# Diagonal blocks packed by ScalarE and sent in one transfer, a shorter layer norm, and a new rule of the planner, in a two-layer trunk on one core

## The chip, the cores and the metric

The kernel runs on one core of a Trainium2 chip. A core has five engines that run their own instruction queues: TensorE (PE, matmuls; PEld is its weight load), VectorE (DVE), ScalarE (ACT), GpSimd (POOL) and SyncE (SP), which here only issues transfers between DRAM and on-chip memory. The metric is the device time of one execution in microseconds (us). The kernel before takes 2513.36 us, the median of three runs of 2513.36, 2511.43 and 2513.53 us.

## What is computed

A decoder trunk of two layers on a sequence of 1024 positions of width 1024, in fp32. Layer 0 mixes the positions by a gated DeltaNet of 8 heads (width 128), layer 1 by an S5 state-space scan. Beside each mixer runs a 4-head attention into 256 memory vectors, and an MLP with squared ReLU follows:

```python
for i in range(DEPTH):                       # 2
    mix, xq = gdn_mixer(x, ...) if i == 0 else s5_mixer(x, ...)
    h = jnp.concatenate([mix, memory_attention(xq, mem, w_kv_mem[i])], -1) @ w_o[i]
    x = layer_norm(DN_ALPHA * x + h, ln1_g[i], ln1_b[i])
    f = jnp.square(jax.nn.relu(x @ mlp_w1[i])) @ mlp_w2[i]
    x = layer_norm(DN_ALPHA * x + f, ln2_g[i], ln2_b[i])

def layer_norm(x, g, b):
    mu = jnp.mean(x, -1, keepdims=True)
    var = jnp.mean(jnp.square(x - mu), -1, keepdims=True)
    return (x - mu) * lax.rsqrt(var + LN_EPS) * g + b

# gated DeltaNet, for one head and chunk by chunk:
#   a_strict = strictly lower part of (beta k) k^T * decay
#   sol = (I + a_strict)^-1 [beta v, beta k exp(gc)]
#   v_new = u - w S ;  o = (q exp(gc)) S + (q k^T * decay) v_new ;  S = S exp(g) + k_dec^T v_new
#   o = o * rsqrt(mean(o^2) + RMS_EPS) * norm_g * silu(z)
```

## The kernel before

**Shape of the work.** A sequence is 8 tiles of 128 positions. Large products use three matmuls per step, high by high, low by high and high by low halves (lines 397, 398 and 399), with the halves made by ScalarE (line 363, 900) and VectorE (line 364, 901). The mixer of layer 0 runs head by head, each head in two halves of four tiles (`hf` is 0 or 1), while the projections of the next heads (tiles `wi`, `wz`, lines 397 to 399) fill TensorE.

**N^T and its transfers.** For each head and half `gdn_keys_out` makes the 128-wide strictly triangular matrices N^T of four tiles (tile `NT`, line 1160: minus the key products times the decay). GpSimd sends the four 32-wide diagonal blocks to DRAM tensor `ntd` with four transfers (line 1163) and the whole tile to `ntf` with one (line 1164). That is 16 calls.

**The inverse.** For each pair of heads `gdn_inverse` loads diagonal blocks back in another layout, solves them in small steps and ends with a run of 16 VectorE instructions on 512 elements (lines 1233 and 1235, in the helper `prod`, called here "the burst"). It reads tiles `X` and `st`, whose loads are lines 1225 to 1227, on SyncE. GpSimd sends the result out (lines 1245, 1246). `gdn_invert_tiles` loads pieces of it per head through SyncE and GpSimd (lines 1272, 1275, 1279) and finishes the 128-wide inverse (tile `iv`) on TensorE (line 1284).

**The recurrence.** `gdn_recur` then steps through the eight tiles of a head. One step is a chain over three engines: `ks` (PE, line 1429), `R` (DVE, line 1431), `pe` (PE, line 1435, needs `iv`), `e` (ACT copy, line 1437), `pS` (PE, line 1441), `S` (DVE, line 1446). Next to it the output of the step is gathered in `po` (PE, lines 1432 and 1447), of which there is one buffer. At the end of a half ScalarE sums the squares (line 1455), VectorE adds a term (line 1456), GpSimd raises to the power -1/2 (line 1457), and ScalarE scales `po` into `on` (line 1460). Only then can the first `po` matmul of the next half be issued. `e`, `R` and `S` share six buffers of one size (tag "S").

**Layer norm.** `layer_norm` either takes statistics by VectorE (lines 509 and 510) or by ScalarE (lines 502 and 505, with small VectorE steps 503 and 506); line 511 makes 1024 (variance + 1e-5), GpSimd raises that to the power -1/2 (line 512), and two passes of VectorE over the tile finish it (lines 522 and 523; lines 514 and 517 for the last tile, which is sent out in two halves by line 518). As the power carries a factor 1/32, the scale vector was multiplied by 32 on ScalarE beforehand (line 2346). In the last MLP the partial sums of a tile are added by line 938.

**What sets the order.** After the program is written down, a planner (`settle`) lists all instructions of all engines in a new order: it keeps a clock per engine and a table of costs and, step by step, takes the instruction that can start first, with preference for the one whose due time is earliest. An instruction becomes ready when those that it depends on are done by the planner's clock, with a lag. Its order is fixed into every engine's queue, in which instructions start in order. So a change of any instruction's cost, engine or dependence moves others on all engines.

Of the kernel before, what the change touches and what calls it, by code (L numbers as in the profile page):

```python
# [10 lines left out]
F32 = mybir.dt.float32  # L11
F32R = mybir.dt.float32r
AF = mybir.ActivationFunctionType
ALU = mybir.AluOpType
AX = mybir.AxisListType

P = 128
# [16 lines left out]
class Trunk:  # L34
    def __init__(self, ctx, tc, a):
        self.tc = tc
        self.nc = nc = tc.nc
        self.a = a
        self.uid = 0
        self.turn = 0  # L40
        self.proj = 0
        self.soon = set()
        self.home, self.fixed = {}, set()
        self.cp = ctx.enter_context(tc.tile_pool(name="cp", bufs=1))
        self.sp = ctx.enter_context(tc.tile_pool(name="sp", bufs=1))
        self.ps = ctx.enter_context(tc.tile_pool(name="ps", bufs=1, space=bass.MemoryType.PSUM))
        self.dp = ctx.enter_context(tc.tile_pool(name="dp", bufs=1, space=bass.MemoryType.DRAM))
        self.ident = self.const("ident", [P, P])
        make_identity(nc, self.ident)
        self.const("pad", [P, 112])  # L50
        self.eps_ln = self.const("eps_ln", [P, 1])
        nc.gpsimd.memset(self.eps_ln, 1024 * 1e-5)
        self.mhalf = self.const("mhalf", [P, 4])
        nc.gpsimd.memset(self.mhalf, -0.5)
        self.half = self.const("half", [P, 4])
        nc.gpsimd.memset(self.half, 0.5)
# [5 lines left out]
    def settle(self, first, last, reach=0.0, ahead=15.0, passes=1, margin=0.0, late=0.0, hold=1e3):  # L62


        E = mybir.EngineType
# [7 lines left out]
        ins = traced[k0:k1]  # L73
        n = len(ins)
# [38 lines left out]
        deps = [set() for _ in ins]  # L113
        reads, writes, users, fresh, cost, port = {}, {}, {}, [], [], []
        opened, follow = {}, [set() for _ in ins]
        for x, i in enumerate(ins):
            new, big, shared = [], 1, i.engine in (E.DVE, E.Pool)
            for out, side in ((False, i.ins), (True, i.outs)):
                for q in side:
# [4 lines left out]
                    b = box(ap)  # L124
# [52 lines left out]
        lag = 0.05  # L177
# [3 lines left out]
        for _ in range(passes):  # L181
# [36 lines left out]
            while len(order) < n:  # L218
# [24 lines left out]
                r, x = first_[1:]  # L243
# [21 lines left out]
                    slots[t].remove(min(slots[t]))  # L265
                    turn[t].remove(nm)
                for y in after[x] + then[x]:
                    same = e == E.PE and ins[y].engine == e
                    ready[y] = max(ready[y], r + (0.0 if x not in deps[y] else busy if same else length + lag + (margin if ins[y].engine == E.PE else 0.0)))
                    wait[y] -= 1  # L270
                    if not wait[y]:
                        open_[ins[y].engine].append(y)
# [220 lines left out]
    def layer_norm(self, y, gb, junk=None, last=None):  # L493
# [1 line left out]
        nc = self.nc  # L495
        st = self.tile("st", [P, 2, 6], F32, "bn")
        halves = y if isinstance(y, list) else [y[:, c * HALF:(c + 1) * HALF] for c in range(2)]
        mv = self.tile("st", [P, 4], F32, "mv")
        if junk is not None:
            s = st.rearrange("p a b -> p (a b)")  # L500
            for c in range(2):
                nc.scalar.activation(junk, halves[c], AF.Copy, accum_out=s[:, c:c + 1])
            nc.vector.tensor_scalar(mv[:, 0:1], s[:, 0:1], s[:, 1:2], -1.0 / 1024, op0=ALU.add, op1=ALU.mult)
            for c in range(2):
                nc.scalar.activation(junk, halves[c], AF.Square, bias=mv[:, 0:1], accum_out=s[:, 4 + c:5 + c])
            nc.vector.scalar_tensor_tensor(mv[:, 2:3], s[:, 4:5], s[:, 5:6], self.eps_ln, op0=ALU.add, op1=ALU.add)
        else:
            for c in range(2):
                nc.vector.bn_stats(st[:, c, :], halves[c])
            nc.vector.bn_aggr(mv[:, 0:2], st)  # L510
            nc.vector.tensor_scalar(mv[:, 2:3], mv[:, 1:2], 1024.0, 1024 * 1e-5, op0=ALU.mult, op1=ALU.add)  # L511
        nc.gpsimd.tensor_tensor(mv[:, 3:4], mv[:, 2:3], self.mhalf[:, 0:1], op=ALU.pow)  # L512
        if last is not None:
            nc.vector.scalar_tensor_tensor(y, y, mv[:, 0:1], gb[0], op0=ALU.subtract, op1=ALU.mult)
            for c in range(2):
# [611 lines left out]
    def gdn_keys_out(self, h, hf):  # L1127
# [28 lines left out]
        for t in range(4):  # L1156
            tt = 4 * hf + t
            c = slice(tt * P, (tt + 1) * P)
            nc.tensor.matmul(pq[:, t, :], kT[:, c], kT[:, c], start=True, stop=True)
        V.scalar_tensor_tensor(n, pq, -1.0, d, op0=ALU.mult, op1=ALU.mult)  # L1160
        for b in range(4):
            q = slice(32 * b, 32 * b + 32)
            nc.gpsimd.dma_start(self.ntd[h, t4, b].rearrange("t j i -> j t i"), n[q, :, q])
        nc.gpsimd.dma_start(self.ntf[h, hf], n)

    def gdn_inverse(self, h0):
# [1173 lines left out]
    def mlp_block(self, i, B, ahead, xd, side, out, more):  # L2340
        new = []

        def done(y, tau):
            if tau == 0:
                self.gb2 = self.load_gb(self.a["ln2_g"][i:i + 1], self.a["ln2_b"][i:i + 1])
                self.nc.scalar.activation(self.gb2[0], self.gb2[0], AF.Copy, scale=32.0)
                if more:
                    new.extend(self.new_xT())
            self.layer_norm(y[tau], self.gb2, self.psum("mm", "jk") if tau in ((), (5, 6))[i] else None, last=out[tau] if tau == 7 and not more else None)
            if tau < 7 or more:  # L2350
                self.nc.sync.dma_start(out[tau], y[tau])
            if more and tau == 7:
                self.last_x(y, new, more(new))
            elif more and tau < 6:
                self.transpose_x(y[tau], tau, new)

        self.mlp_first(i, B, ahead, side)
        self.mlp_second(i, xd, done, side)
        return new
# [87 lines left out]
```

## Time and profile before

| what | us |
|---|---|
| median of the runs | 2513.36 |
| profiled execution, device time | 2512.02 |
| its span on the core | 2510.3 |
| TensorE busy | 2471.1 |
| VectorE busy | 1969.6 |
| ScalarE busy | 1283.0 |
| GpSimd busy | 435.9 |

All times below are microseconds from the start of the profiled execution's span, and its device time is 1.7 us more than the span. TensorE works through all of it, so what counts is where TensorE stands still or has a lower clock. Rows of the timeline read: start, duration, engine, line, operation, output<-input, shape, count and, in brackets, for how long the engine was idle before it and what ended that. Rows of a window read: stretch, its length, then busy time and instruction count of each engine, the granted TensorE clock as a share of full speed, the share of the transfer engines and GB/s.

### The profile page before, as it was taken

What the parts mean: (1) busy time and instruction counts of PE and PEld (TensorE: products, weight loads), DVE (VectorE), ACT (ScalarE), POOL (GpSimd) and SP (SyncE); (2) the same over time, 40 slices, a digit from 0 to 9 for tenths busy, and PEclk for the clock granted to TensorE, in tenths of its full rate; (3) what the DMA queues carried; (4) which work ended last, traced back from release to release, by engine and by line L of the source; (5) the groups of instructions that cost most, each with busy time, mean ns of one, the idle gap of its engine ahead of it and who ended that gap; (6) DMA issues with size and microseconds to landing.
All of it is one profiled execution on the core that took longest, in us unless ns stands there. A gap on an engine that the chain in (4) does not pass through costs nothing.

```text
span 2510.3 us, 36952 instructions
## 1 busy us (share of the span) xinstructions
PE 2471.1 (98%) x12181; PEld 2063.9 (82%) x12181; DVE 1969.6 (78%) x3676; ACT 1283.0 (51%) x2730; POOL 435.9 (17%) x673
## 2 busy tenths in 40 slices
PE   8999999999999999999999999999999999999998
PEld 6888887887887887888888888888887888888886
DVE  7786888777779798879988957786687666578788
ACT  6665555554556576554444244564365555544441
POOL 1232332414002023212210123112011000000000
PEclk9999999999999999999999999999999999999999
DMA  6464585767854567487454489669736434574532
GB/s 211 119 163 125 138 257 135 237 189 226 270 166 157 192 218 236 154 297 240 148 161 134 157 245 301 214 216 331 259 131 206 155 143 164 216 255 133 168 105 97
DMA packets 320769, 481.17 MB, mean 192 GB/s; under 512 B 110225, under 2 KB 141153, under 8 KB 320577
## 3 DMA queue, kind: packets, MB, share of 16 engines
q1 hardware_dynamic: 293056, 423.76, 51.9%
q0 software_dynamic: 25216, 50.86, 6.9%
q10 hardware_dynamic: 2304, 4.20, 0.4%
q8 instruction: 96, 1.57, 0.3%
q14 instruction: 97, 0.79, 0.1%
HBM read 321.91 MB, written 156.73 MB: 191 GB/s over the span
## 4 chain that ended last, share of the span: by engine, by line
PE 87%; DVE 5%; ACT 3%; DMA 2%; issue 2%; POOL 1%; SPq 0%; DVEq 0%; POOLq 0%; ACTq 0%
PE q L398 7%; PE q L397 7%; PE q L399 7%; PE tm L397 4%; PE tm L399 4%; PE tm L398 4%; PE pA L399 3%; PE pA L397 3%; PE pA L398 3%; PE wi L397 3%; PE wi L399 3%; PE wi L398 3%; PE pC L399 2%; PE pC L397 2%; PE pC L398 2%; PE pB L397 2%
## 5 line engine op out<-in xcount | busy, mean ns | idle before, releaser
L397 PE MATMUL q<-wkh,hkh 128*128 128x512 f32 x784 | 306.2, 391 | 0.7 <-ACT G L1886 0.7
L398 PE MATMUL q<-wkl,hkh 128*128 128x512 f32 x784 | 305.9, 390 | 0.5 <-DVE wkl L901 0.5
L399 PE MATMUL q<-wkh,hkl 128*128 128x512 f32 x784 | 305.4, 390 | 0.0
L900 ACT CAST wkh<-wr 128x512 fp32r<-128x512 f32 x168 | 104.9, 624 | 237.5 <-PE q L398 186.2
L512 POOL TENSOR_TENSOR mv<-mv,mhalf 128x1 f32<-128x1 f32 x32 | 26.7, 833 | 858.9 <-DVE mv L511 634.6
L397 PEld LDWEIGHTS q<-wkh,hkh 128*128 128x128 f32 x784 | 147.2, 188 | 32.2 <-ACT G L1886 1.6
L398 PEld LDWEIGHTS q<-wkl,hkh 128*128 128x128 f32 x784 | 147.3, 188 | 31.0 <-DVE wkl L901 1.1
L399 PEld LDWEIGHTS q<-wkh,hkl 128*128 128x128 f32 x784 | 147.2, 188 | 30.5
L901 DVE TENSOR_TENSOR wkl<-wr,wkh 128x512 fp32r<-128x512 f32 x168 | 115.5, 688 | 65.8 <-issue 55.6
L397 PE MATMUL wi<-xTh,wih 128*128 128x512 f32 x384 | 159.9, 416 | 0.2 <-ACT qT L1098 0.2
L398 PE MATMUL wi<-xTl,wih 128*128 128x512 f32 x384 | 152.6, 397 | 0.0
L399 PE MATMUL wi<-xTh,wil 128*128 128x512 f32 x384 | 152.4, 397 | 0.0
L901 DVE TENSOR_TENSOR hkl<-hr,hkh 128x512 fp32r<-128x512 f32 x196 | 133.9, 683 | 0.2 <-ACT hkh L900 0.2
L900 ACT CAST hkh<-hr 128x512 fp32r<-128x512 f32 x196 | 120.8, 616 | 1.3 <-DMA hr<-hd 1.2
L397 PE MATMUL tm<-so 128*128 128x512 f32 x280 | 109.8, 397 | 0.0
L1621 ACT CAST so<-or 128x1024 fp32r<-128x1024 f32 x70 | 72.0, 1049 | 59.5 <-DMA or<-wod 42.0
L1622 DVE TENSOR_TENSOR so<-or,so 128x1024 fp32r<-128x1024 f32 x70 | 84.5, 1220 | 16.1 <-ACT so L1621 16.0
L398 PE MATMUL tm<-so 128*128 128x512 f32 x224 | 88.2, 394 | 0.0
L399 PE MATMUL tm<-so 128*128 128x512 f32 x224 | 87.4, 391 | 0.0
L399 PEld LDWEIGHTS wi<-xTh,wil 128*128 128x128 f32 x384 | 72.7, 189 | 14.8
L397 PEld LDWEIGHTS wi<-xTh,wih 128*128 128x128 f32 x384 | 73.2, 191 | 12.5 <-ACT qT L1098 0.6
L398 PEld LDWEIGHTS wi<-xTl,wih 128*128 128x128 f32 x384 | 73.2, 191 | 11.6 <-issue 0.3
(588 smaller groups left out, 7381.8 us busy)
## 6 DMA issues: line engine op xcount, KB each, us to landing
hr<-hd SPq DMA_DIRECT2D x212, 256.0 KB, 2.8
wr<-in_w_dram SPq DMA_DIRECT2D x56, 512.0 KB, 5.0
hd<-u SPq DMA_DIRECT2D x92, 256.0 KB, 2.0
w1r<-in_w_dram SPq DMA_DIRECT2D x32, 512.0 KB, 3.5
hd<-hid SPq DMA_DIRECT2D x60, 256.0 KB, 2.3
hd<-p SPq DMA_DIRECT2D x60, 256.0 KB, 2.2
w1r<-in_w_dram SPq DMA_DIRECT2D x56, 256.0 KB, 3.6
wir<-in_w_in_dram SPq DMA_DIRECT2D x24, 512.0 KB, 3.9
```

The source lines that it names most:

```text
L397: mm(ps, a[0], b[0], start=start, stop=False, skip_group_check=onto)
L398: mm(ps, a[0], b[1], start=False, stop=False, skip_group_check=onto)
L399: mm(ps, a[1], b[0], start=False, stop=stop, skip_group_check=onto)
L512: nc.gpsimd.tensor_tensor(mv[:, 3:4], mv[:, 2:3], self.mhalf[:, 0:1], op=ALU.pow)
L900: nc.scalar.copy(hi, s)
L901: nc.vector.tensor_tensor(lo, s, f32(hi), op=ALU.subtract)
L1621: nc.scalar.copy(hi, r)
L1622: V.tensor_tensor(lo, r, f32(hi), op=ALU.subtract)
```

## The change

1. In `gdn_keys_out` ScalarE copies the four diagonal blocks of `NT` (32 partitions by 4x32 elements each) into a new tile `pkd`, 128 partitions by 4x32, which takes a buffer of tag "S". GpSimd sends it to `ntd` with one transfer in place of four.
2. `layer_norm` has a tile `mv` of 6 columns. With VectorE's statistics one instruction adds a constant pair (0, 1e-5) to mean and variance, and the factor 1024 is gone; with ScalarE's statistics of whole tiles two small VectorE instructions take the place of one. The multiplication of the second norm's scale vector by 32 on ScalarE is dropped. Two small fills of the constant pair are added at the start.
3. In the last MLP the statistics of tiles 3, 4 and 5 are taken by ScalarE, in place of 5 and 6.
4. The planner treats a dependence between two instructions of one engine other than TensorE, in the last 60 us of its plan and not for transfers, as ready after the first one's busy time plus 0.06 in place of its full length plus the lag.

```diff
@@ -50,6 +50,9 @@
+        self.eps2 = self.const("eps2", [P, 2])
+        nc.gpsimd.memset(self.eps2[:, 0:1], 0.0)
+        nc.gpsimd.memset(self.eps2[:, 1:2], 1e-5)
@@ -265,8 +268,8 @@
-                    same = e == E.PE and ins[y].engine == e
-                    ready[y] = max(ready[y], r + (0.0 if x not in deps[y] else busy if same else length + lag + (margin if ins[y].engine == E.PE else 0.0)))
+                    same = ins[y].engine == e and (e == E.PE or not moves and spot[x] > now - 60.0)
+                    ready[y] = max(ready[y], r + (0.0 if x not in deps[y] else busy + (0.0 if e == E.PE else 0.06) if same else length + lag + (margin if ins[y].engine == E.PE else 0.0)))
@@ -495,7 +498,7 @@
-        mv = self.tile("st", [P, 4], F32, "mv")
+        mv = self.tile("st", [P, 6], F32, "mv")
@@ -503,13 +506,17 @@
-            nc.vector.scalar_tensor_tensor(mv[:, 2:3], s[:, 4:5], s[:, 5:6], self.eps_ln, op0=ALU.add, op1=ALU.add)
+            if isinstance(y, list):
+                nc.vector.scalar_tensor_tensor(mv[:, 1:2], s[:, 4:5], s[:, 5:6], self.eps_ln, op0=ALU.add, op1=ALU.add)
+            else:
+                nc.vector.tensor_scalar(mv[:, 4:5], s[:, 4:5], s[:, 5:6], 1.0 / 1024, op0=ALU.add, op1=ALU.mult)
+                nc.vector.tensor_tensor(mv[:, 1:2], mv[:, 4:5], self.eps2[:, 1:2], op=ALU.add)
         else:
             for c in range(2):
                 nc.vector.bn_stats(st[:, c, :], halves[c])
-            nc.vector.bn_aggr(mv[:, 0:2], st)
-            nc.vector.tensor_scalar(mv[:, 2:3], mv[:, 1:2], 1024.0, 1024 * 1e-5, op0=ALU.mult, op1=ALU.add)
-        nc.gpsimd.tensor_tensor(mv[:, 3:4], mv[:, 2:3], self.mhalf[:, 0:1], op=ALU.pow)
+            nc.vector.bn_aggr(mv[:, 4:6], st)
+            nc.vector.tensor_tensor(mv[:, 0:2], mv[:, 4:6], self.eps2, op=ALU.add)
+        nc.gpsimd.tensor_tensor(mv[:, 3:4], mv[:, 1:2], self.mhalf[:, 0:1], op=ALU.pow)
@@ -1158,9 +1165,11 @@
+        pkd = self.tile("S", [P, 4, 32], F32, "pkd")
         for b in range(4):
             q = slice(32 * b, 32 * b + 32)
-            nc.gpsimd.dma_start(self.ntd[h, t4, b].rearrange("t j i -> j t i"), n[q, :, q])
+            nc.scalar.copy(pkd[q], n[q, :, q])
+        nc.gpsimd.dma_start(self.ntd[h, t4].rearrange("t b j i -> (b j) t i"), pkd)
         nc.gpsimd.dma_start(self.ntf[h, hf], n)
@@ -2343,10 +2352,9 @@
-                self.nc.scalar.activation(self.gb2[0], self.gb2[0], AF.Copy, scale=32.0)
-            self.layer_norm(..., self.psum("mm", "jk") if tau in ((), (5, 6))[i] else None, ...)
+            self.layer_norm(..., self.psum("mm", "jk") if tau in ((), (3, 4, 5))[i] else None, ...)
```

TensorE and SyncE have the same instructions as before. GpSimd issues 48 transfers less, ScalarE has 64 copies more. The line numbers of the changed kernel are higher by 3 to 9: 1233, 1245, 1163, 1272, 1431, 1446 and 1457 are now 1242, 1254, 1172, 1281, 1440, 1455 and 1466. The new order of TensorE differs from the old one from its row 306 on to a place at about 1690 us of the trace before, and is the same from there to the end. Names carry running numbers, which differ between the two programs. In the rows below `pr`, `X`, `st` belong to the burst, `t` and `tv` to the pieces of the inverse, `scr` is any small constant, and `S`, `R`, `ks`, `pS` are those of the recurrence.

**Place 1, GpSimd's queue in the inverse of the second pair of heads.** First the order before, then the new one, from the second of its power instructions on the keys (line 1147, now 1154):

```order
L1147 TENSOR_TENSOR scr_79<-scr_79,half 128x4
L1163 DMA ntd<-NT_4669 32x4x32 x4
L1457 TENSOR_TENSOR scr_79<-scr_79,mhalf 128x4
L1164 DMA ntf<-NT_4669 128x512
L1264 MEMSET iv_4886 128x512
```

```order
L1154 TENSOR_TENSOR scr_82<-scr_82,half 128x4
L1173 DMA ntf<-NT_4696 128x512
L1172 DMA ntd<-pkd_4702 128x4x32
L1281 DMA tv_1965<-t_96 32x4x32 x4
L1284 DMA tv_1965<-t_96 32x4x32 x4
L1173 DMA ntf<-NT_4787 128x512
L1172 DMA ntd<-pkd_4793 128x4x32
L1466 TENSOR_TENSOR scr_82<-scr_82,mhalf 128x4
```

The power of the half's end (line 1457, now 1466) stood behind one group of `ntd`; now it stands behind two of each kind and eight loads of `tv`. On TensorE the last `po` matmul of the half that it belongs to has moved back too, behind 38 more 512-wide matmuls than before (1360 in place of 1322 since the start) and 12 more narrow ones.

**Place 2, VectorE's queue at the burst of the third pair.** Before, and then the new order:

```order
L1103 SCALAR_TENSOR_TENSOR vT_6055<-th_6109,vT_6055 128x512
L1456 SCALAR_TENSOR_TENSOR scr_79<-scr_79 128x4
L1431 SCALAR_TENSOR_TENSOR R_6176<-ks_6174,scr_79,mix_1733 128x128
L1100 SCALAR_TENSOR_TENSOR vT_6056<-cv_6057,scr_79,vT_6056 128x512 x2
L1446 SCALAR_TENSOR_TENSOR S_6234<-S_6150,scr_79,pS_6232 128x128
L1100 SCALAR_TENSOR_TENSOR vT_6056<-cv_6057,scr_79,vT_6056 128x512
L364 TENSOR_TENSOR wil_6471<-wir_6468,wih_6470 128x1024
L1233 TENSOR_TENSOR pr_5538<-X_946_5531,st_950_5577 128x512
```

```order
L1242 TENSOR_TENSOR pr_5573<-X_962_5566,st_966_5612 128x512
L1465 SCALAR_TENSOR_TENSOR scr_82<-scr_82 128x4
L1244 TENSOR_REDUCE X_962_5566<-pr_5573 128x32
L1242 TENSOR_TENSOR pr_967_5613<-X_962_5566,st_966_5612 128x512
L1440 SCALAR_TENSOR_TENSOR R_6211<-ks_6209,scr_82,mix_1744 128x128
L1244 TENSOR_REDUCE X_962_5566<-pr_967_5613 128x32
L1344 TENSOR_TENSOR mix_1744<-qk_6163,Dq_6157 128x512
L1107 SCALAR_TENSOR_TENSOR vT_6091<-cv_6092,scr_82,vT_6091 128x512
L1338 TENSOR_TENSOR gb_6159<-gb_6159,qT_5982 128x512
L1455 SCALAR_TENSOR_TENSOR S_6269<-S_6185,scr_82,pS_6267 128x128
L1107 SCALAR_TENSOR_TENSOR vT_6091<-cv_6092,scr_82,vT_6091 128x512
L1482 SCALAR_TENSOR_TENSOR oT_6327<-ot_6322,ng,thz_5859 128x64x8
```

The burst stood behind `R_6176`, `S_6234` and the split `wil`; now it begins straight behind the counterpart of the row `vT_6055<-th`, and that same `R` (now `R_6211`) comes when all but the last of its 16 instructions are done. On TensorE 41 wide and 12 narrow matmuls now stand between that `ks` and its `pe`; before, 33 wide and 9 narrow ones stood between the next `ks` and the `pe` that waited for the burst.

**Place 3, VectorE's queue behind the burst of the first pair.** In the order before, six instructions stand between the `R` at the burst's end (`R_3128`) and the first `S` behind it (`S_3206`); in the new order 23 rows stand between the two (`R_3147` and `S_3227`). The last of them and the `S`:

```order
L1107 SCALAR_TENSOR_TENSOR qT_3107<-cv_3108,scr_82,qT_3107 128x512 x2
L1126 SCALAR_TENSOR_TENSOR D_3169<-gb_3167,scr_82 128x128 x4
L1107 SCALAR_TENSOR_TENSOR qT_3107<-cv_3108,scr_82,qT_3107 128x512
L1098 MEMSET cv_3713 128x3
L1159 TENSOR_TENSOR D_3169<-D_3169,scr_82 128x512
L1110 SCALAR_TENSOR_TENSOR qT_3107<-th_3255,qT_3107 128x512
L1167 SCALAR_TENSOR_TENSOR NT_3198<-kk_3197,D_3169 128x512
L1107 SCALAR_TENSOR_TENSOR vT_3302<-cv_3304,scr_82,vT_3302 128x512 x2
L637 TENSOR_TENSOR ws_2948<-ws_2947,ws_2948 128x512
L1455 SCALAR_TENSOR_TENSOR S_3227<-S_3122,scr_82,pS_3225 128x128
```

Work on later heads (`qT`, `D`, `NT`, `vT`) and a weight sum (`ws`) thus moved ahead of that `S`.

At the very end of VectorE's queue the last tile's small step of line 511 (now 518) stood behind the first full pass (line 514, now 521); now it stands ahead of it. The pass of line 522 on the tile before has moved ahead of the last but one addition of line 938 (now 945), and both passes of line 523 (now 530) still open stand ahead of the last addition.

More of the change, by code (lines that the diff above doesn't have):

```diff
@@ L2345, in done @@
                 self.gb2 = self.load_gb(self.a["ln2_g"][i:i + 1], self.a["ln2_b"][i:i + 1])
[L2346 removed]
                 if more:
                     new.extend(self.new_xT())
[L2349 removed]
+            self.layer_norm(y[tau], self.gb2, self.psum("mm", "jk") if tau in ((), (3, 4, 5))[i] else None, last=out[tau] if tau == 7 and not more else None)
             if tau < 7 or more:
```

## The prediction

> **What bounds the kernel now.** The page comes first: which engine is full.
>
> ```profile
> span 2510.3 us, 36952 instructions
> PE 2471.1 (98%) x12181; PEld 2063.9 (82%) x12181; DVE 1969.6 (78%) x3676; ACT 1283.0 (51%) x2730; POOL 435.9 (17%) x673
> ```
>
> TensorE is busy for all but 39.2 us of the span (2510.3 - 2471.1), and the change takes no matmul away. So it can win from those 39 us, from stretches in which TensorE's clock is low, and nowhere else; what it may lose has no such limit. The second view is therefore TensorE's waits.
>
> ```profile
> PE ba L1011 <- ACT xTh L993: 7.9, 2, 7.2
> PE po L1432 <- ACT on L1460: 4.3, 5, 2.4
> PE pe L1435 <- DVE R L1431: 3.0, 1, 3.0
> PE pS L1441 <- ACT e L1437: 1.0, 2, 0.6
> ```
>
> The first (total, times, longest) is the start of the program, which stays. The next two have their longest waits in the recurrence, where the order changes. A scan of windows over the span finds the two spots, and the third view is windows of 2 us there.
>
> ```profile
> 434.00:436.00 2.00, 0.76 (x4) 0.55 (x4) 1.97 (x3) 1.70 (x4) 2.00 (x4) 1.00 0.51 121
> 436.00:438.00 2.00, 1.18 (x5) 0.61 (x4) 1.98 (x5) 0.00 (x0) 1.98 (x3) 1.00 0.22 45
> 438.00:440.00 2.00, 0.46 (x4) 0.46 (x5) 0.21 (x1) 1.65 (x7) 2.00 (x5) 1.00 0.33 94
> 440.00:442.00 2.00, 2.00 (x10) 1.81 (x9) 1.32 (x2) 1.97 (x8) 2.00 (x4) 0.55 0.81 227
> 442.00:444.00 2.00, 2.00 (x9) 1.67 (x9) 1.89 (x7) 0.89 (x6) 2.00 (x5) 0.60 0.60 131
> 572.00:574.00 2.00, 0.12 (x1) 0.00 (x0) 2.00 (x4) 0.98 (x1) 0.00 (x0) 1.00 0.01 3
> 574.00:576.00 2.00, 0.56 (x3) 0.37 (x3) 2.00 (x5) 0.67 (x2) 0.73 (x1) 1.00 0.83 264
> 576.00:578.00 2.00, 1.32 (x8) 1.16 (x9) 2.00 (x5) 1.10 (x2) 1.58 (x3) 0.68 0.95 317
> 578.00:580.00 2.00, 2.00 (x9) 1.81 (x9) 2.00 (x4) 0.71 (x2) 1.73 (x3) 0.50 1.00 211
> ```
>
> Place 1: from 434 to 440 TensorE works 2.40 of 6 us, so 3.6 are lost, and for the next 4 us it is granted 0.55 and 0.60 of its clock, which costs 2 x 0.45 + 2 x 0.40 = 1.7 more: 5.3 in all. Place 2: 572 to 578, 4.0 idle, then 1.32 x 0.32 + 2 x 0.50 = 1.4 in clock: 5.4 in all. So both pauses cost about 10.7 us, 0.43% of the time.
>
> **Place 1: what the pause hangs on, and what the change does to it.** The timeline around it, GpSimd and TensorE apart:
>
> ```profile
> 434.77 2.23 POOL L1163 DMA_DIRECT2D ntd<-NT  x4
> 437.02 1.30 POOL L1457 TENSOR_TENSOR scr<-scr,mhalf 128x4 f32<-128x4 f32 x1
> 439.54 0.49 PE L1432 MATMUL po<-S,gb 128*128 128x128 f32 x2 [2.36 <-ACT on L1460]
> ```
>
> Four issues of `ntd` hold GpSimd for 2.23 us, the power of line 1457 comes behind them, `on` on ScalarE behind that, and `po` waits 2.36 for `on`. The cost of those transfers, and of the other kind from the same tile, is in the groups of GpSimd:
>
> ```profile
> L1163 POOL DMA_DIRECT2D ntd<-NT x64 | 35.3, 557 | 66.3 <-DVE NT L1160 64.2 <-DMA ntd<-NT 1.9 <-DVE bz L1294 0.2
> L1164 POOL DMA_DIRECT2D ntf<-NT x16 | 9.2, 574 | 0.0
> ```
>
> One issue takes 0.56 to 0.57 for 32 partitions as for 128. The merged transfer isn't in this trace; its bounds are 0.56 (line 1164, also 128 partitions) and 2.23 (the old four together), and I take 0.57, as row 1164 is its nearest. So the removed issues free 48 x 0.56 = 27 us of GpSimd, which is 83% idle: worth nothing but at such a place. And here the new order puts more ahead of the power: two `ntf`, two `ntd` and eight `tv`, 12 x 0.56 = 6.7 us in place of 2.2. By itself that would make the pause 4.5 longer. But TensorE's last `po` of this half also moves back, behind 38 wide matmuls (0.23 us each, their pitch in place 2 below: 8.7) and 12 narrow ones (an estimate of 0.1 each, from their number of columns: 1.2), so by 9.9 us; GpSimd is then ready first. What I find left in the new order, by the same counting of each engine's queue with the trace's durations: VectorE needs 19.6 us between an `R` and an `S` across the burst where TensorE has 18.9 of work, which with the hand-over makes `ks` 1.1 late; 0.3 at a `pe`; 1.3 at the products that make `iv`, whose loaded pieces come later through the longer queue; and 0.3 at `po`. Sum 3.0, in pieces. I expect no lowered clock, so place 1 goes from 5.3 to 3.0: -2.3. Its ends are -5.3 (all four covered) and +2.2 (GpSimd's 4.5 longer chain in full).
>
> **Place 2.** VectorE and TensorE of the timeline, and the loads that the burst waits for (first their durations and the start of the last, then issue to landing):
>
> ```profile
> 554.36 0.69 DVE L1103 SCALAR_TENSOR_TENSOR vT<-th,vT 128x512 f32<-128x512 f32 x1 [0.29 <-ACT th L1102]
> ...
> 556.22 0.35 DVE L1431 SCALAR_TENSOR_TENSOR R<-ks,scr,mix 128x128 f32<-128x128 f32 x1 [0.24 <-PE ks L1429]
> ...
> 563.06 2.01 DVE L1233 TENSOR_TENSOR pr<-X,st 128x512 f32<-128x512 f32 x2
> ...
> 572.89 1.28 DVE L1235 TENSOR_REDUCE X<-pr 128x32 f32<-128x512 f32 x2
> ...
> 574.68 0.35 DVE L1431 SCALAR_TENSOR_TENSOR R<-ks,scr,mix 128x128 f32<-128x128 f32 x1
> 571.51 0.39 PE L398 MATMUL wz<-xTl,wzh 128*128 128x512 f32 x1
> 571.73 0.39 PE L399 MATMUL wz<-xTh,wzl 128*128 128x512 f32 x1
> 575.08 0.49 PE L1435 MATMUL pe<-R,iv 128*128 128x128 f32 x2 [2.96 <-DVE R L1431]
> L1227 SPq DMA_DIRECT2D X<-t x8: 617/634/2860, 120.9 to 554.1; - x8
> DMA to landing us min/median/max: 2.3/2.8/4.7
> ```
>
> The burst takes 563.06 to 574.1, 11.0 us, `R` is late behind it, and `pe` waits 2.96. In the new order the burst starts straight behind the row at 554.36, that is by 555.1 for VectorE; but its last load is issued at 554.1 and lands 2.8 later, so it starts at 556.9. The `R` that ran at 556.22 now comes with one reduction (0.6) of the burst left, about 0.1 for line 1456 added: 556.9 + 11.0 - 0.6 + 0.1 = 567.4. Row to row an `R` gives its `pe` 0.4 later (574.68, 575.08): 567.8. TensorE reaches that `pe` after 41 wide and 12 narrow matmuls from a `ks` that ended near 555.9: 9.4 + 1.7 = 11.1, so at 567.0. Wait 0.8. In the next step VectorE has `R`, `vT` and `oT`, about 2.2 us, against 1.4 of TensorE's work: 1.4 more, in two pieces. So 2.2 idle in place of 4.0, and no half clock: from 5.4 to 2.2, -3.2. The ends are -5.4 (no wait) and +3 (the loads land 4.7 after their issue, the longest of that row, and the next steps carry the delay on).
>
> **Place 3: a new wait.** Before, the burst of the first pair ended just in time:
>
> ```profile
> 290.06 0.36 DVE L1431 SCALAR_TENSOR_TENSOR R<-ks,scr,mix 128x128 f32<-128x128 f32 x1
> 290.92 0.38 PE L1435 MATMUL pe<-R,iv 128*128 128x128 f32 x2
> 291.79 0.69 DVE L1103 SCALAR_TENSOR_TENSOR kT<-th,kT 128x512 f32<-128x512 f32 x1
> ```
>
> `pe` came 0.86 behind `R`, with no wait. The new order's 23 rows between that `R` and the next `S` are, start to start, eight convolution steps at 0.68 (each a little over that of 291.79), three like that row at 0.62, a split of 1.1, 1.2 for `D`, three passes of 0.6 and 0.7 of small ones: 12.1 us of VectorE. TensorE has 38 wide and 15 narrow matmuls there (8.7 + 1.65), with the hand-overs from `R` and to `S` 11.15. With 0.25 for the hand-over TensorE waits 1.2; the following step (7.5 against 6.9) adds 0.5. So +1.7; its ends are 0 (VectorE runs ahead as before) and +3.4 (both twice as long).
>
> **The end.** After TensorE's last matmul VectorE is alone:
>
> ```profile
> 2489.52 0.69 DVE L938 TENSOR_TENSOR y<-tm,y 128x512 f32<-128x512 f32 x1 [0.24 <-PE tm L399]
> 2492.24 0.69 DVE L938 TENSOR_TENSOR y<-tm,y 128x512 f32<-128x512 f32 x1 [0.71 <-PE tm L399]
> ...
> 2500.17 1.46 POOL L512 TENSOR_TENSOR mv<-mv,mhalf 128x1 f32<-128x1 f32 x1 [5.08 <-DVE mv L506]
> 2503.65 0.21 DVE L510 BATCH_NORM_AGGREGATE mv<-bn 128x2 f32<-128x12 f32 x1
> 2505.39 0.55 POOL L512 TENSOR_TENSOR mv<-mv,mhalf 128x1 f32<-128x1 f32 x1 [3.76 <-DVE mv L511]
> 2505.97 1.41 DVE L517 SCALAR_TENSOR_TENSOR y<-y,mv,gb 128x512 f32<-128x512 f32 x2 [0.73 <-POOL mv L512]
> ```
>
> From the aggregate (2503.65) to the end of the last pass (2507.38) it takes 3.73. In the new order the power starts beside the first pass: aggregate 0.2, step 0.15, pass 1.28, then the last pass 1.41, together 3.0, if the power takes 0.55 as at 2505.39. But the power that ran beside a full pass took 1.46 (2500.17) and came 0.4 behind that pass; then 3.5. The Trainium skill says the same in "GPSIMD Engine Reference", Specifications: GpSimd's memory interface is shared with VectorE, with contention from VectorE instructions of two memory inputs; by that rule the whole term would be 0.2 of gain in place of 0.7. I take 3.5, the row. The aggregate itself comes earlier, since VectorE no longer idles for ScalarE's sums of the tile before: TensorE delivers a sum every 2.72 (2489.52, 2492.24), so the next addition can run at 2494.95, and from there VectorE has, start to start, 0.6, 0.75, 0.25, 0.15 and 1.2 for that tile's statistics and pass, 0.6 and 0.7 for the next sum, two passes of 1.2, 0.6 and 0.7 for the last: 2502.9 in place of 2503.65. With the 0.2 above it is -0.9; ends -1.5 (the power not held up) and +0.4 (the sums of tile 5 on ScalarE come late for the passes). The earlier ScalarE statistics replace VectorE's for two tiles more and one less, in a stretch that TensorE bounds.
>
> **At nothing:** the two fills (at the start, while TensorE waits 7.2 for something else), the dropped scaling on ScalarE, and SyncE's reordering. The 64 copies are not free by right. Nearest row, a ScalarE copy of 128 partitions by 128:
>
> ```profile
> L1437 ACT COPY e<-pe 128x128 f32<-128x128 f32 x64 | 17.0, 266 | 43.0 <-PE pe L1435 40.9 <-DVE tv L1298 1.7
> ```
>
> 64 x 0.27 = 17 us on an engine that is busy 51%; cover is ScalarE's idle half. Without cover each call (four copies) would delay the next `e` by 1.1. I take 0, and price the other end as a rival.
>
> **Sum.** -2.3 - 3.2 + 1.7 - 0.9 = -4.7, from the profiled 2512.02 to 2507.3. The median of the runs stands 1.34 above the profiled one, so 2508.7 against 2513.36. A measurement of this kernel can tell about 0.2%, 5.0 us, from no change: the forecast lies at that bound, and I give 2508.5.
>
> **Rivals.**
> - *Both pauses go, and no new wait comes.* For it: every new wait is 1.4 or less, from counted queues in which a few tenths decide. Against: place 3 needs VectorE a whole microsecond faster. -5.3 - 5.4 - 0.9 = -11.6: 2501.8.
> - *The pauses only move.* For it: in the same rows the burst's 11.0 us still has to fit between two steps, and GpSimd has 6.7 us ahead of the power. Idle as before, the end's 0.9 won: 2512.5. Here belongs the clock. At place 1 it fell although the longest single wait was 2.36; if the new waits at places 1 and 3 do that too, 1.7 each comes back, and 2508.7 becomes 2512.1. The Trainium skill, "TensorE: Matmul & The Clock Gate", Why this matters for your kernels, asks for gaps over about 3 us before the clock halves; by it neither new place would fall, but place 1 in this trace fell with less.
> - *Slower: the copies stand in front of `e`.* ScalarE starts its queue in order, and the new order has copies of `pkd` just ahead of `e` in several calls; a copy waits for `NT` on VectorE (line 1160), and `e` with it. Twelve of the 16 calls lie beside a running recurrence. At 1.1 each that is +13: 2521.9. It decides from 0.4 each (4.7 / 12), and makes the kernel measurably slower from 0.8. Against: TensorE waited for `e` for 0.6 at most before (the fourth row of its waits), and the planner knows of the copies.
>
> **How the numbers follow.** Forecast (2505 to 2511.5) 0.48, of it 0.25 beyond the 0.2%; larger gain 0.16; moved pauses (2510 to 2515) 0.20; slower 0.16. Faster is 0.25 + 0.16 = 0.41, same 0.23 + 0.20 = 0.43, slower 0.16. The range leaves a tenth at each side: 2501 to 2518.
>
> **What would show it.** Right: no window of 2 us near 430 to 450 or 560 to 585 with a clock under 0.9, `ntd` with 16 issues of about 0.57, new short waits of `ks` on `S` near 300, the last pass ending about 3.1 us after the first pass of the last tile starts (3.48 before). Wrong: `pe` or `pS` waiting for `e` in many places (the copies), a pause over 2 us at a new place, or more idle TensorE time in all than 36 us.

## The result: slower by 0.35%

The changed kernel takes 2521.22 us, the median of six runs (2518.04 to 2525.10), against 2513.45 us of the kernel before on the same chip (six runs, 2511.04 to 2516.41). The ratio is 1.0035, with an interval of 1.0024 to 1.0047. So it is 7.8 us slower; the forecast was 2508.5, with a range that ended at 2518.

The profiled execution of the changed kernel is the slowest of its six, 2525.1 us. Its page, first the engines and then GpSimd's transfer queue (packets, MB, share of 16 transfer engines):

```profile
span 2523.4 us, 37000 instructions
PE 2476.7 (98%) x12181; PEld 2062.4 (82%) x12181; DVE 1973.4 (78%) x3677; ACT 1304.0 (52%) x2800; POOL 417.9 (17%) x627
q0 software_dynamic: 23680, 50.85, 7.7%
```

TensorE stands still for 46.7 us (2523.4 - 2476.7), where it was 39.2. The two profiled spans lie 13.1 us apart, further than the medians. The queue's row of before is the next one: fewer packets take a larger share now, for the same bytes.

```profile
q0 software_dynamic: 25216, 50.86, 6.9%
```

**Where the time came from.** Each matmul form is given its median distance to the next matmul, and these are summed along TensorE's queue. The time at which a kernel has done a given sum, less that of before, is what it has lost by then. Where two kernels issue matmuls in different orders this is good to about 1 us, and single executions of one order differ by that much in a stretch as well. In stretches of the time of before:

```
stretch of before, us    changed kernel   e1: the same, tiles as before   e2: before, tiles moved 32 bytes
   0 -  255                  +1.7              +0.1                           -1.3
 255 -  300  (place 3)       +1.0              +1.1                            0.0
 300 -  430                  +2.3              +1.9                            0.0
 430 -  471  (place 1)       -0.9              -1.7                           +1.1
 471 -  550                  +0.5              +0.5                           -0.2
 550 -  590  (place 2)       -4.3              -4.3                           +0.3
 590 -  930                  -0.1              -1.9                           +0.5
 930 - 1000                  +1.8              +2.3                           -0.2
1000 - 1460                  +0.1              +0.1                           +0.2
1460 - 1620  (S5 scan)      +10.0              +0.4                          +10.0
1620 - last matmul           +1.5              +1.0                           +1.1
sum                         +13.6              -0.4                          +11.4
```

(e1 and e2 are experiments, below.) The loss is not in the delta-net, where the new order is, but in the S5 scan of layer 1, 1460 to 1620 us. Windows of 40 us there (columns as in the section on the profile before), first of the kernel before, then of the changed one:

```profile
1500.00:1540.00 40.00, 40.00 (x237) 35.30 (x236) 26.88 (x50) 18.95 (x30) 13.06 (x20) 1.00 0.99 288
1540.00:1580.00 40.00, 40.00 (x235) 35.22 (x234) 27.68 (x52) 21.16 (x34) 14.77 (x22) 1.00 1.05 336
1580.00:1620.00 40.00, 40.00 (x231) 35.11 (x230) 31.85 (x68) 20.77 (x37) 4.05 (x5) 1.00 0.65 178
```

```profile
1500.00:1540.00 40.00, 38.95 (x221) 33.94 (x220) 26.35 (x49) 18.37 (x29) 13.88 (x21) 1.00 1.01 274
1540.00:1580.00 40.00, 38.16 (x210) 33.58 (x209) 26.53 (x49) 19.35 (x30) 12.08 (x18) 0.96 1.02 288
1580.00:1620.00 40.00, 36.38 (x214) 31.66 (x212) 23.97 (x47) 15.33 (x25) 7.14 (x9) 1.00 0.86 231
```

Before, TensorE never stood still, while the transfer engines were full: a busy share of 0.99 and 1.05. Now the same engines are as full for longer (0.86 in place of 0.65 in the last row) and move less per time (288 in place of 336 GB/s), and TensorE idles 6.5 us in these 120 and has a lower clock in the second row. What it waits for there, by the changed kernel's waits from 1460 to 1620:

```profile
PE py L1980 <- DMA H<-h1d: 4.6, 3, 1.8
PE p L1954 <- DMA s5t<-ud: 1.9, 1, 1.9
```

The kernel before has in that stretch one wait, of 0.2. `H` is loaded through GpSimd's queue. The transfers of that stage, KB each and median us from issue to landing, before and then now:

```profile
tab<-tabd POOLq DMA_DIRECT2D x32, 256.0 KB, 5.4
s5t<-zd POOLq DMA_DIRECT2D x8, 512.0 KB, 11.5
H<-h1d POOLq DMA_DIRECT2D x16, 256.0 KB, 11.5
```

```profile
tab<-tabd POOLq DMA_DIRECT2D x32, 256.0 KB, 8.1
s5t<-zd POOLq DMA_DIRECT2D x8, 512.0 KB, 12.8
H<-h1d POOLq DMA_DIRECT2D x16, 256.0 KB, 13.3
```

Same loads, same bytes, yet the transfers are slower.

**The suspect.** The constants lie ahead of all tiles in on-chip memory, each in a slot of a multiple of 32 bytes. The kernel before has one that nobody uses, line 50: `self.const("pad", [P, 112])`. With it the built program has all its large tiles at multiples of 512 bytes. The new constant `eps2` of part 2 takes one more slot, and all 3276 tiles of 2 KB and more begin 32 bytes behind such a multiple:

```
                 before     changed
first tile        18432      18464
gb                23552      23584
s5t              144384     144416
```

### The profile page after: what moved, and what is told of

It is laid out like the page before. It is cut to its first block, busy times and chain, and to the rows that moved or that the text cites. A ratio compares the mean times of both kernels' runs of the same rounds, so it can differ in the third digit from the quotient of the medians.

```text
span 2523.4 us, 37000 instructions
## 1 busy us (share of the span) xinstructions
PE 2476.7 (98%) x12181; PEld 2062.4 (82%) x12181; DVE 1973.4 (78%) x3677; ACT 1304.0 (52%) x2800; POOL 417.9 (17%) x627
## 4 chain that ended last, share of the span: by engine, by line
PE 79%; DVE 6%; DMA 6%; issue 4%; ACT 3%; POOL 1%; SPq 1%; POOLq 0%; DVEq 0%; ACTq 0%
PE q L401 7%; PE q L400 7%; PE q L402 7%; PE tm L400 4%; PE tm L402 4%; PE tm L401 4%; PE pA L402 3%; PE pA L400 3%; PE pA L401 3%; PE wi L400 2%; PE wi L401 2%; PE wi L402 2%; PE pC L402 2%; PE pC L401 2%; PE pC L400 2%
## 5 line engine op out<-in xcount | busy, mean ns | idle before, releaser
L402 PE MATMUL tm<-so 128*128 128x512 f32 x224 | 87.8, 393 | 0.0
```

The lines of the kernel that those rows point to most:

```text
L402: mm(ps, a[1], b[0], start=False, stop=stop, skip_group_check=onto)
```

## The experiments

No kernel here leaves out or changes anything of the computation.

**e1 to e4: the address, the order, the packing.** Four kernels on one chip. e1 is the changed kernel with the unused constant smaller by one slot, so that the tiles lie where they lay before:

```diff
-        self.const("pad", [P, 112])
+        self.const("pad", [P, 104])
```

> The changed kernel with the padding constant shortened from 112 to 104 numbers, so that all tiles of 2 KB and more lie at multiples of 512 bytes again, as in the kernel before; every engine's order is that of the changed kernel. If the 32-byte shift of all tiles is what slowed the transfers of the S5 stage (theory A), the 10 us lost there come back: 2510 to 2514 us, and the GpSimd queue's packets fall from 132 ns on average to about 109. If the new order is what costs (theory B), it stays at 2519 to 2523 us. If the S5 stage only had a bad draw of transfers (theory C), both this and the changed kernel scatter over 2515 to 2523.

e2 is the kernel before with that constant larger by one slot, so that its tiles lie as the changed kernel's do. Every engine's order is that of before, here and in e5 to e11:

```diff
-        self.const("pad", [P, 112])
+        self.const("pad", [P, 120])
```

> The kernel before with the padding constant lengthened from 112 to 120 numbers: all tiles of 2 KB and more move to 32 bytes behind a multiple of 512, nothing else changes, and every engine's order is that of the kernel before. Theory A: slower by 6 to 11 us, 2519 to 2524 us, lost between 1480 and 1670 us. Theories B and C: 2513 us, as before.

e3 is the kernel before with the packing alone (part 1 of the change), and the tiles where they were:

```diff
+        pkd = self.tile("S", [P, 4, 32], F32, "pkd")
         for b in range(4):
             q = slice(32 * b, 32 * b + 32)
-            nc.gpsimd.dma_start(self.ntd[h, t4, b].rearrange("t j i -> j t i"), n[q, :, q])
+            nc.scalar.copy(pkd[q], n[q, :, q])
+        nc.gpsimd.dma_start(self.ntd[h, t4].rearrange("t b j i -> (b j) t i"), pkd)
```

> The kernel before with the packed diagonal blocks alone (64 ScalarE copies, one transfer for four), tiles at multiples of 512 bytes; its planner, layer norm and last MLP are those of before. Theory A: only the delta-net stage differs, whose sum in the changed kernel's trace was within 1 us of before at 600 us: 2511 to 2516 us. Theory B, if the packing's new order costs: 2518 us or more.

e4 is e1 without the packing, that is parts 2 to 4 alone.

> The changed kernel with the four old transfers of the diagonal blocks in place of the packing, tiles at multiples of 512 bytes: layer norm, statistics of tiles 3 to 5, and the planner's new rule remain. Theory A: 2510 to 2514 us, 0.5 to 1 us of it won at the end, after TensorE's last matmul. Theory B, if the new rule's order costs: 2517 us or more.

Measured:

```
kernel                                      median us  runs   ratio to before (2512.93, 27 runs)
e1  changed, tiles where they were            2512.30    11   0.9998  [0.9990, 1.0007]
e2  before, tiles moved by 32 bytes           2522.75     5   1.0036  [1.0023, 1.0048]
e3  before with the packing                   2513.01    11   0.9999  [0.9990, 1.0008]
e4  changed without the packing, tiles as e1  2512.01    11   0.9999  [0.9989, 1.0008]
```

e2 changes not one instruction and has the whole loss; e1 has all of the change but the address and no loss. The windows of e1 and e2 in the S5 scan agree:

```profile
1540.00:1580.00 40.00, 40.00 (x227) 34.94 (x226) 30.98 (x58) 20.75 (x33) 14.77 (x23) 1.00 1.01 322
1580.00:1620.00 40.00, 39.84 (x230) 34.76 (x229) 29.57 (x64) 21.13 (x36) 2.21 (x3) 1.00 0.61 163
```

```profile
1540.00:1580.00 40.00, 38.40 (x218) 33.45 (x217) 27.78 (x53) 19.48 (x31) 12.87 (x19) 1.00 1.00 295
1580.00:1620.00 40.00, 38.70 (x231) 33.85 (x230) 26.96 (x53) 17.32 (x28) 6.66 (x9) 1.00 0.82 226
```

In e1 TensorE is full again and the load of the transfer engines falls off as before; in e2 it idles as in the changed kernel. e2's waits in the stretch are the changed kernel's too: `H`, by line 1971 of its own, and `s5t`:

```profile
PE py L1971 <- DMA H<-h1d: 3.0, 2, 1.9
PE p L1945 <- DMA s5t<-ud: 1.8, 2, 1.6
```

So the loss of 7.8 us is the address of the tiles, and the change without it is worth nothing that these runs can tell.

Two things more. The packets of GpSimd's queue, 109.3 ns on average before and 131.9 in the changed kernel, take 117.7 in e1 and not the 109 that I expected; e3, with the packing alone, has 115.4, so the queue's new mix of packets accounts for most of that. And the new order in the delta-net is the packing's: in stretches as above e3 has about +1 at place 3, -1 at place 1 and -4 at place 2, and e4 has nothing at any of the three.

**e5 to e8: how far, and which tiles.** e5 is e2 with a shift of 256 bytes in place of 32:

```diff
-        self.const("pad", [P, 112])
+        self.const("pad", [P, 176])
```

> The kernel before with the padding constant lengthened from 112 to 176 numbers: all tiles of 2 KB and more lie 256 bytes behind a multiple of 512, in the same order. If what counts is where each 512-byte piece starts against lines of 256 bytes (theory A1), this is as fast as before: 2512 to 2514 us. If the whole 512 bytes count (A2), it is slow as with 32 bytes: 2520 to 2524 us.

e6, e7 and e8 move a part of the tiles by 32 bytes: a small filler is taken from the memory just ahead of the first tile of a tag and, in e6 and e7, one of 480 bytes behind the group, so that the rest stays. e6 moves the six 16 KB buffers of tag "xT", of which the S5 scan takes `s5t` and the projections take `xTh` and `xTl`; e7 those of tag "h1", with `H` and `G`; e8 everything from tag "gb" on.

```diff
+        n = {"xT": 8, "gb": 120}.get(tag)     # e6;  e7: {"h1": 8, "raw": 120};  e8: {"gb": 8}
+        if n and tag not in self.begun:
+            self.sp.tile([P, n], F32, tag="pad" + tag, name="pad" + tag, bufs=1)
+        self.begun.add(tag)
```

> The kernel before with the six 16 KB buffers of tag xT alone moved by 32 bytes, all other tiles at multiples of 512; same order. These hold s5t, into which GpSimd's queue loads the reading matrices in 512-byte pieces (eight transfers of 512 KB) and from which the drives go. If s5t carries the loss: 2517 us or more. If G, H and tab carry it: 2512 to 2515 us.

> The kernel before with the seven 2 KB buffers of tag h1 alone moved by 32 bytes; same order. These hold most of G1 (2 KB pieces) and H1 (512-byte pieces), 32 loads of 256 KB on GpSimd's queue. If the loss goes by 512-byte pieces: 2515 to 2518 us, if these loads don't carry it: 2512 to 2514 us.

> The kernel before with all tiles from tag gb on (tags gb, h5, h2, h3, h4: the rotation tables tab, the matrices on their way out to DRAM, y of the scan) moved by 32 bytes; tags scr, h1, raw, w1 and xT stay at multiples of 512; same order. If each group carries its share of the 9 us: 2515 to 2518 us; if s5t or h1 carries it all: 2512 to 2514 us.

Measured, against 2514.07 of before (15 runs): e5 2513.35, ratio 0.9999 [0.9990, 1.0007]; e6 2543.27, 1.0116 [1.0102, 1.0130]; e7 2535.46, 1.0086 [1.0072, 1.0100]; e8 2533.23, 1.0074 [1.0062, 1.0087].

e5 says that a shift as such does nothing; 256 bytes are free. e6 to e8 were no clean division: each costs more than moving everything did. What they add is not in the S5 scan (e6 loses 6.8 there, e7 0.2 and e8 1.2, where e2 loses 10.0) but all along the products. Windows of 100 us in the last MLP, of before, of e2 and of e6:

```profile
2000.00:2100.00 100.00, 100.00 (x443) 82.84 (x442) 61.06 (x94) 53.75 (x94) 0.00 (x0) 1.00 0.43 153
```

```profile
2000.00:2100.00 100.00, 100.00 (x443) 82.81 (x442) 62.41 (x98) 53.96 (x94) 0.00 (x0) 1.00 0.41 148
```

```profile
2000.00:2100.00 100.00, 100.00 (x431) 80.51 (x430) 59.49 (x92) 53.21 (x93) 0.00 (x0) 1.00 0.41 146
```

Nothing waits and the clock is full, but e6 does 431 matmuls where the others do 443: 232 ns each in place of 226. By form, every one of e6 to e8 whose two operands lie in differently moved tiles is slower (`wg<-xTh,wgl` goes from 227 to 233 ns from start to start in e6). A few with both operands alike are slower too: in e7 and e8 `q<-wkh,hkh` (234 and 232), which runs between unlike ones, and in e6 `tm<-so` (231), for which I have no reason. When all tiles are moved alike, as in e2 and in the changed kernel, no form is slower. So this second effect is a product of the experiment, and no part of the change's loss.

For the transfers e6 still tells something. Around the scan GpSimd's queue moves the same 7200 packets in all these kernels. Their times, summed and divided by the 16 engines, are 71.5 us before, 81.8 in e2, 82.6 in the changed kernel, 70.2 in e1 and 69.4 in e5. In e6 it is 77.7, in e7 71.8, in e8 71.3. Kernels with all tiles at multiples of 256 bytes scatter from 68 to 73, so `s5t`, the one tile of tag "xT" that this queue loads there, brings some 6 of the 10 us, and neither of the other two groups shows any by itself; where the other 4 us come from stays open. Nor is all of e6's 6.8 us of loss there due to transfers: TensorE waits 2.9 us for them in e6 and 5.1 in e2, and some 3 us of e6's loss are spread over matmuls that follow each other without a pause at full clock, which fits the second effect. e6's waits from 1460 to 1640 us:

```profile
PE py L1975 <- DMA H<-h1d: 2.5, 4, 1.1
PE p L1949 <- DMA s5t<-ud: 0.4, 1, 0.4
```

SyncE's queue shows little of all this. Over the whole program the mean of one of its packets is 71.2 ns before, 71.0 in e2 and 71.4 in the changed kernel. Its packets around the scan, some 19 400, take 87.8 us before, 89.9 in e2 and 90.7 in the changed kernel: 2 to 3% more, where GpSimd's queue takes 14 to 16% more. e7 and e8, in which GpSimd's queue is not slower, have 89.8 and 90.2 there.

**e9 to e11: the size of the line.** e9 and e10 move all tiles by 128 and by 64 bytes (`[P, 144]` and `[P, 128]`); e11 moves tag "xT" alone by 256 (e6's edit with `{"xT": 64, "gb": 64}`).

> The kernel before with the padding constant at 144 numbers: all tiles of 2 KB and more 128 bytes behind a multiple of 512, same order. With 32 bytes the loss was 9 us, with 256 none. If a piece that starts off a 256-byte line costs whatever the distance: 2519 to 2523 us and about 82 us of transfer time on the GpSimd queue in the S5 stage, as with 32. If the cost grows with how far a piece reaches over the line: between, 2515 to 2518 us. If 128 is a line too: 2513 us and 70 us.

> The same with the padding constant at 128 numbers: all tiles 64 bytes behind a multiple of 512. If only the 256-byte line counts: 2519 to 2523 us. If multiples of 64 are enough: 2513 us.

> The kernel before with the six buffers of tag xT alone moved by 256 bytes. Moved by 32 bytes alone they slowed 512-wide matmuls against unmoved tiles from 227 to 233 ns and cost 29 us in all. If the matmul's cost hangs on the operands' distance modulo 256 or less, both effects vanish: 227 ns and 2513 us. If it hangs on the distance modulo 512, the matmuls stay at 233 ns and about 22 us are lost, with the S5 stage as fast as before.

Measured, with the time of GpSimd's 7200 packets around the scan as above and the mean of one of its packets over the whole program (e9 to e11 against 2512.71 of before, 25 runs):

```
tiles moved by            median us   ratio to before             queue, us   packet, ns
0    before                                                         71.5       109.3
32   e2                     2522.75   1.0036 [1.0023, 1.0048]       81.8       120.6
64   e10                    2518.18   1.0019 [1.0009, 1.0028]       79.9       119.6
128  e9                     2517.37   1.0017 [1.0007, 1.0026]       77.9       116.8
256  e5                     2513.35   0.9999 [0.9990, 1.0007]       69.4       108.8
256  e11, tag "xT" alone    2512.92   0.9998 [0.9987, 1.0008]       70.6       109.8
```

So what counts is the start within a line of 256 bytes: off it, packets take 7 to 11 ns more, and the S5 scan, which runs its transfer engines full, cannot hide it. TensorE's waits for transfers from 1460 to 1640 us go the same way: 5.1 us in e2, 4.3 in e10, 2.0 in e9, 0.8 in e11, none in e5 and before. e10 lies in neither of the two ranges that I gave it. e9 lies in the middle one of its three, but the reason given there, a cost that grows with how far a piece reaches over the line, is not borne out: 32 bytes cost more than 128. e11 also clears the products: with operands 256 bytes apart the window from 2000 to 2100 us has 442 matmuls, before 443.

The Trainium skill speaks of such a line: "DMA: Bandwidth & Descriptors", How a descriptor splits into AXI transactions, says that a piece that does not start at a 256-byte boundary has its first transaction start at the boundary below, and that the unused bytes are paid for too. An estimate by it: a piece of 512 bytes, as those of `H` and `s5t` are (128 elements of 4 bytes), takes three transactions in place of two when moved by 32, 64 or 128, and two when moved by 256. The traces agree in which shifts cost and which do not. They do not agree in how much: counting bytes fetched, 128 should cost most of the three, and it cost about half of what 32 did. The Trainium skill words its rule for bytes that are read, and in these loads the moved end is the one that is written. Why 32 bytes cost most, and why SyncE's transfers are nearly spared, no run here tells.

## Why the prediction was wrong

**The step that failed** is the first item under "At nothing": the two fills of the constant pair "at the start, while TensorE waits 7.2 for something else". I costed the constant by the instructions that fill it and not by the memory that it takes. Moving the tiles by its 32 bytes costs 9.8 us without the rest of the change (e2, 2522.75 against 2512.93). The sum of -4.7 had no term for it, and no rival spoke of the S5 scan, where the kernel's transfer engines were full in the very trace that I read.

The sum itself, without that term, is tested by e1: 2512.30 against 2512.93, a ratio between 0.9990 and 1.0007. A gain of 4.7 would be 0.9981, so the sum was too large as well. Its terms:

- *Place 1, forecast 3.0 us idle in pieces and no lowered clock (-2.3).* The idle time and the clock came as said. In the changed kernel the pause of 434 to 444 is gone, and this is the stretch in one window:

```profile
430.00:458.00 28.00, 25.12 (x142) 20.51 (x140) 25.40 (x54) 16.07 (x52) 16.61 (x26) 1.00 0.69 201
```

  2.9 us idle at a clock of 1.00. The pieces are others than I named: `po` waits 0.94, but the two longest of the rest are `wz`, a projection that waits for ScalarE to empty its buffer (`vT`), 0.83 and 0.42. Idle and clock make -2.4 against before; the table of losses, -0.9 (e1: -1.7). There are five interruptions in place of three; what makes up the difference between the two figures these traces do not tell.
- *Place 2, forecast 2.2 idle and no half clock (-3.2).* It gave more, -4.3 in both kernels. I had let the burst wait for its last load, 2.5 behind the row of `vT`. In the changed kernel it starts straight behind that row, with no wait for a load:

```profile
559.12 0.69 DVE L1110 SCALAR_TENSOR_TENSOR vT<-th,vT 128x512 f32<-128x512 f32 x1 [0.28 <-ACT th L1109]
559.73 2.02 DVE L1242 TENSOR_TENSOR pr<-X,st 128x512 f32<-128x512 f32 x2
```

  So the 0.8 at `pe` did not come. Of the 1.4 of the next step 0.71 came, `ks` waiting for `S`. From 560 to 584 the kernel idles 0.8 us, all of it here:

```profile
576.00:580.00 4.00, 3.17 (x19) 2.27 (x19) 4.00 (x6) 2.80 (x5) 3.57 (x7) 1.00 0.62 146
```

  Two of this term's figures do not follow from their rows: 12 narrow matmuls are taken at 1.7, where place 1 has 12 at 1.2, and 2.2 of VectorE against 1.4 of TensorE makes 0.8, not 1.4.

- *Place 3, forecast +1.7 from `ks` waiting for `S`.* The size was near, +1.0 (e1: +1.1); the mechanism was not. In e1, whose times are close to those of before, `ks` behind the 23 rows does not wait at all. TensorE has been stopped earlier, by a projection that waits for ScalarE:

```profile
294.71 0.40 PE L402 MATMUL wi<-xTh,wil 128*128 128x512 f32 x1
296.69 0.51 PE L400 MATMUL wi<-xTh,wih 128*128 128x512 f32 x1 [1.58 <-ACT qT L1105]
303.19 0.38 PE L1450 MATMUL pS<-e,kdl 128*128 128x128 f32 x2
304.79 0.38 PE L1438 MATMUL ks<-S,kT 128*128 128x128 f32 x2
```

  Before, the same two matmuls of `wi` were:

```profile
295.69 0.40 PE L399 MATMUL wi<-xTh,wil 128*128 128x512 f32 x1
296.24 0.50 PE L397 MATMUL wi<-xTh,wih 128*128 128x512 f32 x1 [0.15 <-ACT qT L1098]
```

  With the recurrence's matmuls moved back, TensorE is through with the first of them 1.0 earlier (294.71 in place of 295.69), and ScalarE starts `qT`, which empties the buffer, 0.5 later (295.97 in place of 295.50). I counted VectorE's queue against TensorE's and left ScalarE's out. e3 has the same wait (1.6) and e4 has not (0.2): it comes with the packing's order.
- *New waits I did not foresee.* From 300 to 430 the loss is 2.3 (e1: 1.9), also in e3 and not in e4; in the changed kernel 1.6 of it are waits, on `e` (0.9), `S` (0.5) and `tv` (0.2). From 930 to 1000 it is 1.8 (e1: 2.3). There TensorE waits for VectorE (`pA` on `a1l`): before once, 1.7; in the changed kernel three times, 2.9 in all, at full clock; in e1 once, 2.0, at an earlier place, and the clock falls behind it, which costs 1.6 more (18.03 us of work at 0.91 in the last row of this document). From 50 to 690 us e1 gains 2.3 of the 3.8 that places 1 to 3 were to bring, and 930 to 1000 takes as much back. This is the rival "the pauses only move", 2512.5, against e1's 2512.30.
- *The end, forecast -0.9.* In e1 9.42 us lie between the end of the last matmul and the end of the span, 9.94 before: -0.5. The part from the aggregate to the end came as taken, beside a power that ran along with a full pass and took long. In the changed kernel:

```profile
2516.86 0.21 DVE L517 BATCH_NORM_AGGREGATE mv<-bn 128x2 f32<-128x12 f32 x1
2517.30 1.28 DVE L521 SCALAR_TENSOR_TENSOR y<-y,mv,gb 128x1024 f32<-128x1024 f32 x1
2517.44 1.56 POOL L519 TENSOR_TENSOR mv<-mv,mhalf 128x1 f32<-128x1 f32 x1 [5.24 <-DVE mv L518]
2519.03 1.41 DVE L524 SCALAR_TENSOR_TENSOR y<-y,mv,gb 128x512 f32<-128x512 f32 x2 [0.44 <-POOL mv L519]
```

  From 2516.86 to 2520.44 it is 3.58, where I took 3.5; the rest of the term, an aggregate 0.75 earlier, came only in part.
- *The copies and the merged transfer.* Groups of e1:

```profile
L1171 ACT COPY pkd<-NT 32x128 f32<-32x128 f32 x64 | 18.9, 295 | 5.7 <-DVE NT L1167 5.0
L1172 POOL DMA_DIRECT2D ntd<-pkd x16 | 12.3, 767 | 26.1 <-ACT pkd L1171 26.1
```

  A copy takes 0.295 in place of 0.27, an issue 0.77 in place of 0.57: nearer to the transfer of whole partitions than to four old ones, as taken. The rival "slower: the copies stand in front of `e`" gave 2521.9, almost the time measured, and was nevertheless wrong: between 250 and 650 us of the changed kernel TensorE waits 1.2 us in three pieces for an `e` at `pS` (1.0 in two before), and e3, which has all the copies, is no slower than before. A time that fits is no proof of a mechanism.

Of the signs that the prediction named, three held: no low clock at places 1 and 2, `ntd` with 16 issues (of 0.77, not 0.57), and the last pass ending 3.14 after the first pass of the last tile starts (2517.30 to 2520.44). The `ks` near 300 did not, and the one for "wrong" that came was the idle time of TensorE: 46.7 us, above 36 (e1: 36.6).

## What to carry to other kernels

A constant or a small tile costs more than its instructions when it moves what is allocated behind it: compare the tiles' start addresses of both programs, modulo 256 bytes, before any timing argument, above all where a stage keeps its transfer engines full. An unused constant named `pad` is a sign that somebody has aligned something; add a slot and shrink the pad by as much. And where an order is replanned, count all queues that hold buffers TensorE needs, the one that empties them too: place 3 came to wait for ScalarE, and the 2.3 us that e1 had gained by 690 us were lost again behind 930 us, by a wait for VectorE and the clock that fell behind it.

## What the runs showed of the hardware that was not expected

- Transfers of GpSimd's queue are slower with tiles that start off a 256-byte line: 117 to 121 ns a packet in place of 109, for shifts of 128, 64 and 32 bytes (e9, e10, e2); 256 is free (e5, 108.8). Transfers issued by SyncE stayed at 71 ns a packet.
- A 512-wide fp32 matmul whose moving and stationary tile differ by 32 bytes in their offset has a pitch (start to start) of 233 in place of 227 ns, 2.6% (e6). If all tiles are moved alike (e2), or those of one tag by 256 (e11), it is 227. Over the program e6 lost 29 us, most of it all along the products.
- TensorE's clock can fall after a wait of 2.0 us, that of `pA` in e1:

```profile
951.62 0.50 PE L402 MATMUL pA<-xB,a1l 128*128 128x512 f32 x1 [1.97 <-DVE a1l L587]
940.00:960.00 20.00, 18.03 (x73) 14.43 (x72) 16.89 (x44) 12.41 (x23) 6.63 (x13) 0.91 0.71 230
```

  At place 3 the wait of 1.58 in e1 left it at 1.00. The Trainium skill, "TensorE: Matmul & The Clock Gate", Why this matters for your kernels, speaks of gaps over about 3 us; this row is against it, as place 1 of before was.
